# One modulation block of a diffusion layer, moved from the latent periods into the context's weight stream

## The chip, the cores and the metric

The kernel runs on one core of one Trainium2 chip. The metric is the device time of one execution in microseconds (us); the time before is the median of three runs. Engines are named as the profile names them: PE (TensorE matmuls) and PEld (its weight loads, which overlap the matmuls), DVE (VectorE), ACT (ScalarE), POOL (GpSimd), SP (SyncE, which issues nearly all DMAs). Line numbers such as L854 are lines of the kernel before.

## The reference

One layer over 512 latent tokens and 256 context tokens, width D = 2048, all in float32:

```python
mod = silu(c) @ w_ada + b_ada                  # six vectors of 2048: sh1, sc1, g1, sh2, sc2, g2
xm  = rmsnorm(x, n1) * (1 + sc1) + sh1         # latent; the context has its own sh1 and sc1
p_c = xm_ctx @ w_in[:, state columns]          # context: keys and values only
p   = xm @ w_in                                # latent: all columns
out = concat(rwkv(p, state_c), retention(p, state_c)) @ w_out
x   = x + g1 * rmsnorm(out, n2)
h   = rmsnorm(x, n3) * (1 + sc2) + sh2
y   = (silu(dwconv3x3(h @ w_gate)) * (h @ w_up)) @ w_down
x   = x + g2 * rmsnorm(y, n4)
```

The RWKV group is a delta-rule scan with one state per head and direction: the context's 256 tokens first, in four batches of heads, then the latents' 512, in eight batches, which start from the context's final states. The retention group works in chunks of 128. The modulation block that this change moves is sh2, a product of one vector of 2048 with a 2048 x 2048 matrix (16.8 MB of weights). It is needed first where h is made, long after both places where it is computed.

## The kernel before, in words

A float32 product is split in three: the weights w = hi + lo and the activations x = hi + lo, each part in a format of TensorE's single-pass matmul, and hi·hi, hi·lo and lo·hi are accumulated. The weights come through one generator, `stream` (L184). It loads a block of 4 x 128 rows (256 KB) by a DMA on SP into one of `rbufs` = 3 raw buffers, and `cut` makes hi with an ACT cast (L203) and lo with a DVE subtraction (L204) into one of `wbufs` = 3 pairs of buffers, then issues the load that refills the ring. A consumer takes one k-step of 128 rows at a time and issues its three matmuls (a triple below). Of one block, a context tile of the joint kind (`both`, L552) makes four triples of 512 and four of 256 columns, a retention tile of the context (`ret_context`, L675) four of 256, and a latent tile four of 512.

`start` makes the norms and the first products. `mixers` (L284) then runs four context batches and eight latent periods. A batch is `rw_prep`, `rw_fill` (decays, transposes, products, and the triangular solve `rw_solve` with 30 dependent steps of two DVE instructions, from the transposes of L1188 to those of L1200) and `rw_chain` (the scan). `fill` (L293) interleaves the projections' k-steps with the batch's steps in program order; how many tiles go with which batch stands in `TILES`. While the chain of one batch runs, the next batch's preparation runs beside it. The framework that builds the program then orders each engine's instructions by its own estimate of when their inputs are there, so an instruction can run far ahead of, or behind, its place in the code. At run time each engine, and SP's queue of DMA issues, goes through its list in order.

The six modulation vectors are computed in two ways. sh1 and sc1 are made on TensorE in `start`. The other four go through `ada_rest` (L828), one vector each in a different stage: a block of weights is loaded, DVE multiplies it by one element of silu(c) per partition and adds it to an accumulator (L852 opens a group, L854 continues it), and at the end of a group matmuls with a vector of ones sum over the partitions and a DVE addition puts the bias on (L859). For sh2 (`m` = 1), `mixers` opens a pool `ada2` after the context and pulls one unit (one DMA of 256 KB, 128 partitions x 512 columns, and one DVE instruction) for every `ADA` = 20 steps of projection, ten k-steps of a latent tile. There are 64 units in four groups of 16.

In the context the work pool gives the small state tiles `w` three buffers (`self.nw`, L288); the last step of a chain writes the new state into such a tile and stores it from there (L1318).

Of the kernel before, what the change touches and what calls it, by code (L numbers as in the profile page):

```python
# [9 lines left out]
F32 = mybir.dt.float32  # L10
F32R = mybir.dt.float32r
AF = mybir.ActivationFunctionType
ALU = mybir.AluOpType
# [3 lines left out]
D = 2048  # L17
KT = D // 128
# [11 lines left out]
PK_K, PK_A, PR_K, PLNW, PLNB, PW0, PA0, PNPRE, PNPOST, PFPRE, PFPOST, PCONV, PBADA, PFCB, PFCW = range(15)  # L30
# [17 lines left out]
OUT = [0.0, 1.0]  # L48
ADAR = 0.9
ADAW = 3  # L50
ADA = 20
EV = 4
ORDER = ((False, 0), (True, 2), (True, 3), (True, 0), (True, 1), (False, 1), (False, 2), (False, 3))
LAG = 2
# [13 lines left out]
def pull(steps, n=None):  # L68

    while n is None or n > 0:  # L70
        if next(steps, None) is None:
            return
        n = n and n - 1


def drain(steps):
    for _ in steps:
        pass


def merge(*streams, lead=False):


    at = [0.0] * len(streams)
    left = list(range(len(streams)))
    done = 0.0
    while left:
        i = min(left, key=lambda j: at[j])
        t = next(streams[i][0], None)
        if t is None:  # L90
            left.remove(i)
# [12 lines left out]
def fill_time(ctx):  # L104
    return 2 * (Y["d0"] + Y["d1"] + (1 if ctx else 2) * Y["d2"]) + 30 * Y["s0"] + Y["s1"] + Y["s2"] + Y["s3"] + (0 if ctx else Y["b"])


def chain_time(ctx):
    return 4 * (Y["c0"] + Y["c1"]) + 3 * Y["c2"] if ctx else 8 * (Y["c0"] + Y["c1"] + Y["c3"]) + Y["o1"] + Y["o2"]


class Kernel:
# [71 lines left out]
    def stream(self, srcs):  # L184

        nc, w = self.nc, self.wk
        blocks = (src[:, k0:k0 + w] for src in srcs for k0 in range(0, src.shape[1], w))
        raws, parts = [], []

        def load():  # L190
            src = next(blocks, None)
            if src is not None:
                n, m = src.shape[1:]
                raw = self.wp.tile([128, w, 128], F32, name="raw", bufs=self.rbufs)
                nc.sync.dma_start(raw[:, 0:n, 0:m], src)
                raws.append((raw, n, m))

        def cut():
            if raws:
                raw, n, m = raws.pop(0)  # L200
                hi = self.wp.tile([128, w, 128], F32R, name="whi", bufs=self.wbufs)
                lo = self.wp.tile([128, w, 128], F32R, name="wlo", bufs=self.wbufs)
                nc.scalar.copy(hi[:, 0:n, 0:m], raw[:, 0:n, 0:m])  # L203
                nc.vector.tensor_tensor(lo[:, 0:n, 0:m], raw[:, 0:n, 0:m], hi[:, 0:n, 0:m].bitcast(F32), op=ALU.subtract)  # L204
                parts.append((hi, lo, n, m))
                load()

        for _ in range(self.rbufs):
            load()
        for _ in range(self.wbufs - 1):  # L210
            cut()
        while parts:
            hi, lo, n, m = parts.pop(0)
            for k in range(n):
                if k == 1:
                    cut()
                yield hi[:, k, 0:m], lo[:, k, 0:m]
# [66 lines left out]
    def mixers(self, es, esw, esx, esc):  # L284

        self.done = None
        self.work, self.nt2 = self.pool(esc, "work_ctx", reuse_waits="tile"), NTC
        self.nw, self.nsv = 3, 3  # L288
        self.bw = self.pool(esc, "batch_ctx", reuse_waits="tile")
        tiles = self.ctx_tiles + self.lat_tiles  # L290
        esa, ada = ExitStack(), iter(())

        def fill(todo, *parts):  # L293

            nonlocal ada
            n, gone, done = sum(c for _, _, c in todo), 0, 0.0
            steps = chain.from_iterable(f() for _, f, _ in todo)
            for work, unit in parts:
                for t in work:
                    done += t * unit  # L300
                    while gone + 2 <= min(done, 1.0) * n:
                        t = next(steps)
                        pull(ada, (gone + t) // ADA - gone // ADA)
                        gone += t
            drain(steps)

        def take(n):
            nonlocal tiles
            todo, tiles = tiles[:n], tiles[n:]
            return todo  # L310

        nc_ = NP // 2
        prep = prep_time()
        B = self.context(0)
        drain(self.rw_prep(B))
        fill(take(TILES[0]), (self.rw_fill(B), 1 / fill_time(True)))
        for i in range(nc_):
            streams = [(self.rw_chain(B), chain_time(True), EARLYC)]
            if i + 1 < nc_:
                B = self.context(i + 1)  # L320
                streams.append((chain(self.rw_prep(B), self.rw_fill(B)), prep + fill_time(True), 1.0))
            fill(take(TILES[1 + i]), (merge(*streams, lead=True), 1.0))
        esx.close()
        esc.close()
        ap = self.pool(esa, "ada2", side="right", reuse_waits="tile")
        ada = self.ada_rest(ap, 1, 1, 2)
        self.work, self.nt2 = self.pool(es, "work", reuse_waits="tile"), NT2
        self.nw, self.nsv = NW, NSV
        self.bw = self.pool(es, "batch", reuse_waits="tile")

        self.ul = self.work.tile([128, 2, 2, 128], F32R, name="ul")
        self.nc.gpsimd.memset(self.ul.bitcast(F32), 0.0)
        batches = [self.latent(p) for p in range(NP)]
        for B, after in zip(batches, batches[1:]):
            B.next = after
        B = batches[0]
        fill(take(TILES[nc_ + 1]), (chain(self.rw_prep(B), self.rw_fill(B)), 1 / (prep + fill_time(False))))

        def period(B, p):
            streams = [(chain(self.rw_chain(B), self.rw_out(B)), chain_time(False), EARLY)]  # L340
            if p + 1 < NP:
                B = batches[p + 1]
                streams.append((chain(self.rw_prep(B), self.rw_fill(B)), prep + fill_time(False), 1.0))
            return B, merge(*streams, lead=True)

        for p in range(NP):
            todo = take(len(tiles) if p == NP - 1 else TILES[nc_ + 2 + p])
            B, steps = period(B, p)
            fill(todo, (steps, 1.0))
        pull(ada)  # L350
        esa.close()
        esw.close()
        es.close()

# [100 lines left out]
    def start(self):  # L455

        nc, a, sp = self.nc, self.a, self.sp
# [6 lines left out]
        for k in range(KT):  # L464
            for i, (pool, name, n, tag) in enumerate(kinds):
                t = pool.tile([128, n], F32, name=f"{tag}r{k}", tag=f"{tag}{k}")
# [36 lines left out]
        for k in range(KT):  # L503
# [4 lines left out]
            for i in range(len(tiles)):  # L508
                hi, lo = (w[:, k % SW] for w in ws[i])
# [3 lines left out]
                    nc.tensor.matmul(o, hi, xl, start=False, stop=False)  # L513
                    nc.tensor.matmul(o, lo, xh, start=False, stop=(last and k == KT - 1))
        first, self.ctx_tiles, self.lat_tiles = self.tiles()
        wst = self.stream([self.win(t) for ts, _, _ in first + self.ctx_tiles + self.lat_tiles for t in ts])
        self.wst = chain([next(wst)], wst)

        def out(ctx, i):
# [221 lines left out]
    def retention(self, h):  # L741
        nc, a, rp = self.nc, self.a, self.rp

        def tile(name, n=L, bufs=2):
            return rp.tile([128, n], F32, name=name, bufs=bufs)
# [9 lines left out]
        raw = []  # L755
# [28 lines left out]
        q, k = rot  # L784
# [15 lines left out]
        t = score(0)  # L800
        yield 1
        for c in range(4):
# [4 lines left out]
            t = nx  # L807
# [16 lines left out]
        nc.vector.tensor_tensor(o, po, g, op=ALU.mult)  # L824
        self.split(o, self.hh[NP + h], self.hl[NP + h])
        yield 1

    def ada_rest(self, pool, m, nk=2, bufs=3):  # L828

# [627 lines left out]
```

## Time and profile before

| | |
|---|---|
| median of three runs | 3343.24 us (3338.36 to 3350.64) |
| profiled execution, its own time | 3337.66 us |
| its span, first to last instruction | 3335.8 us |
| mean granted TensorE clock | 0.974 of 2.4 GHz |
| PE / PEld busy | 3158.3 / 2502.3 us |
| DVE / ACT / POOL busy | 2083.9 / 1121.2 / 240.6 us |
| read from HBM | 399.75 MB, 129 GB/s over the span with what is written |

The kernel's stages follow one another in the span: start to 195 us, context to about 645 us, latents to about 1500 us, retention and output projection to about 1830 us, ConvGLU to the end. A busy PE isn't a PE at its peak, since matmuls overlap and their ends are modelled.

### The profile page before, as it was taken

To read this page: it belongs to the slowest core of one execution; us is meant where nothing else is said; L and a number is where in the kernel's file an instruction comes from. 1 tells how busy PE (TensorE), PEld (TensorE's weight loads), DVE (VectorE), ACT (ScalarE), POOL (GpSimd) and SP (SyncE) were. 2 spreads that over 40 slices of the span, in tenths; PEclk is the share of its full clock that TensorE was granted. 3 is DMA by queue.
4 is the path that set the end of the run, shared out by engine and by line. 5 is a ranking of instruction groups with operands and counts; after the bars stand their busy time and mean duration, and the time that the engine had idled before them with its cause. 6 is when DMAs were issued, how large, how long until landed. Compare 5 with 4: busy or idle time off the path is not lost.

```text
span 3335.8 us, 50268 instructions
## 1 busy us (share of the span) xinstructions
PE 3158.3 (95%) x19672; PEld 2502.3 (75%) x19672; DVE 2083.9 (62%) x3562; ACT 1121.2 (34%) x1954; POOL 240.6 (7%) x382
## 2 busy tenths in 40 slices
PE   6999999989999999998998899999999999999997
PEld 3688888866767676676777688888888888788885
DVE  4474767788787878765668856335643555345544
ACT  3333245434344344333233432223322232223322
POOL 0000011101111111111210100000000000000001
PEclk9999998999999999999999899999999999999998
DMA  8832223442243433326778434333433333333342
GB/s 295 271 103 77 76 83 93 134 147 94 85 146 102 146 97 95 123 71 224 248 232 271 152 106 132 104 101 95 146 93 98 101 95 108 115 106 95 96 143 103
DMA packets 197724, 433.64 MB, mean 130 GB/s; under 512 B 25360, under 2 KB 49680, under 8 KB 197488
## 3 DMA queue, kind: packets, MB, share of 16 engines
q1 hardware_dynamic: 197488, 430.45, 40.7%
q8 instruction: 154, 2.52, 0.3%
q14 instruction: 82, 0.67, 0.1%
HBM read 399.75 MB, written 30.61 MB: 129 GB/s over the span
## 4 chain that ended last, share of the span: by engine, by line
PE 46%; DMA 4%; issue 3%; DVE 2%; POOL 1%; ACT 0%; SPq 0%; POOLq 0%; ACTq 0%; DVEq 0%
PE gbank L179 14%; PE gbank L181 14%; PE gbank L180 14%; DMA adaw<-ada 2%; DVE adacc L854 1%; POOL y L915 0%; DMA raw<-w_out 0%; DMA rxs<-ret_t 0%; DMA om<-o_mix 0%; PE gbank L903 0%; PE gbank L904 0%; PE gbank L905 0%; PE gbank L736 0%; PE gbank L737 0%; PE gbank L738 0%
## 5 line engine op out<-in xcount | busy, mean ns | idle before, releaser
L161 DVE TENSOR_TENSOR wlo<-raw,whi 128x1024 fp32r<-128x1024 f32 (+1 forms) x336 | 342.3, 1019 | 617.5 <-ACT whi L160 608.5
L160 ACT CAST whi<-raw 128x1024 fp32r<-128x1024 f32 (+1 forms) x336 | 297.2, 889 | 901.0 <-PE gbank L180 866.4
L179 PE MATMUL gbank<-hh,whi 128*128 128x512 f32 x1376 | 535.5, 389 | 0.0
L181 PE MATMUL gbank<-hh,wlo 128*128 128x512 f32 x1376 | 535.4, 389 | 0.0
L180 PE MATMUL gbank<-hl,whi 128*128 128x512 f32 x1376 | 535.3, 389 | 0.0
L203 ACT CAST whi<-raw 128x512 fp32r<-128x512 f32 (+2 forms) x320 | 210.8, 659 | 490.2 <-PE gbank L548 215.8
L549 PE MATMUL gbank<-xh,wlo 128*128 128x512 f32 (+1 forms) x896 | 368.1, 411 | 7.8 <-DVE wlo L204 7.8
L547 PE MATMUL gbank<-xh,whi 128*128 128x512 f32 (+1 forms) x896 | 368.9, 412 | 0.0
L548 PE MATMUL gbank<-xl,whi 128*128 128x512 f32 (+1 forms) x896 | 365.8, 408 | 0.0
L204 DVE TENSOR_TENSOR wlo<-raw,whi 128x512 fp32r<-128x512 f32 (+2 forms) x320 | 235.0, 737 | 106.0 <-ACT whi L203 90.1
L181 PEld LDWEIGHTS gbank<-hh,wlo 128*128 128x128 f32 x1376 | 258.3, 188 | 53.8
L180 PEld LDWEIGHTS gbank<-hl,whi 128*128 128x128 f32 x1376 | 258.3, 188 | 53.7
L179 PEld LDWEIGHTS gbank<-hh,whi 128*128 128x128 f32 x1376 | 258.3, 188 | 53.6
L181 PE MATMUL gbank<-dh,wlo 128*128 128x512 f32 x704 | 278.1, 395 | 0.4 <-DVE wlo L161 0.4
L179 PE MATMUL gbank<-dh,whi 128*128 128x512 f32 x704 | 278.0, 395 | 0.0
L180 PE MATMUL gbank<-dl,whi 128*128 128x512 f32 x704 | 277.8, 395 | 0.0
L944 DVE SCALAR_TENSOR_TENSOR cacc<-grid,fprm,cacc 128x512 f32<-128x512 f32 x352 | 264.2, 751 | 9.7 <-ACT cacc L941 1.1
L854 DVE SCALAR_TENSOR_TENSOR adacc<-adaw,sc,adacc 128x512 f32<-128x512 f32 x240 | 187.8, 783 | 74.0 <-DMA adaw<-ada 72.2
L549 PEld LDWEIGHTS gbank<-xh,wlo 128*128 128x128 f32 (+1 forms) x896 | 169.8, 190 | 51.4 <-DVE wlo L204 10.1
L547 PEld LDWEIGHTS gbank<-xh,whi 128*128 128x128 f32 (+1 forms) x896 | 170.2, 190 | 40.0 <-issue 4.8
L548 PEld LDWEIGHTS gbank<-xl,whi 128*128 128x128 f32 (+1 forms) x896 | 170.0, 190 | 37.1 <-issue 2.2
L181 PEld LDWEIGHTS gbank<-dh,wlo 128*128 128x128 f32 x704 | 132.4, 188 | 33.4 <-DVE wlo L161 1.2
(307 smaller groups left out, 4977.8 us busy)
## 6 DMA issues: line engine op xcount, KB each, us to landing
raw<-w_in SPq DMA_DIRECT2D x284, 256.0 KB, 3.0
adaw<-ada SPq DMA_DIRECT2D x192, 256.0 KB, 3.3
raw<-w_gate SPq DMA_DIRECT2D x88, 512.0 KB, 3.6
raw<-w_up_ffn SPq DMA_DIRECT2D x88, 512.0 KB, 3.6
ada<-ada SPq DMA_DIRECT2D x64, 512.0 KB, 6.1
raw<-w_down SPq DMA_DIRECT2D x64, 512.0 KB, 3.6
raw<-w_out SPq DMA_DIRECT2D x32, 512.0 KB, 5.4
adaw<-ada SPq DMA_DIRECT2D x32, 512.0 KB, 4.6
```

Source lines behind the costliest of these rows:

```text
L160: nc.scalar.copy(hi[:, 0:n, 0:m], raw[:, 0:n, 0:m])
L161: nc.vector.tensor_tensor(lo[:, 0:n, 0:m], raw[:, 0:n, 0:m], hi[:, 0:n, 0:m].bitcast(F32), op=ALU.subtract)
L179: self.nc.tensor.matmul(o, hi, xh(k), start=(k == 0), stop=False)
L180: self.nc.tensor.matmul(o, hi, xl(k), start=False, stop=False)
L181: self.nc.tensor.matmul(o, lo, xh(k), start=False, stop=(k == nk - 1))
L203: nc.scalar.copy(hi[:, 0:n, 0:m], raw[:, 0:n, 0:m])
L204: nc.vector.tensor_tensor(lo[:, 0:n, 0:m], raw[:, 0:n, 0:m], hi[:, 0:n, 0:m].bitcast(F32), op=ALU.subtract)
L547: self.nc.tensor.matmul(o, hi, xh[k], start=(k == 0), stop=False)
L548: self.nc.tensor.matmul(o, hi, xl[k], start=False, stop=False)
L549: self.done = self.nc.tensor.matmul(o, lo, xh[k], start=False, stop=(k == KT - 1))
L854: nc.vector.scalar_tensor_tensor(acc, w[:, k], c, acc, op0=ALU.mult, op1=ALU.add)
L944: nc.vector.scalar_tensor_tensor(acc, grid[:, dy:dy + 8, dx:dx + 64], cw[:, f, i:i + 1], acc, op0=ALU.mult, op1=ALU.add)
```

## The change

The units of sh2 become blocks of the weight stream while it serves the context tiles. An entry of the stream can now be a pair of a source and a function `use`; such an entry is loaded into a raw buffer like a block of weights, and when it comes to the front, `use` runs on the raw buffer in place of the cast and the subtraction, a load is issued, and the next entry is taken. The context tiles have 112 blocks. `among` leaves the first 8 and the last 8 of them alone (`AGAP`) and puts 64 units behind two of every three of the 96 between. A unit is now 2 rows of k by 256 columns, so it holds as many bytes as before (256 KB), in runs of 1 KB instead of 2 KB, and takes two DVE instructions of 256 columns instead of one of 512. There are eight groups of eight units; a group ends with two matmuls with ones and one DVE addition. The accumulator `adacc` (1 KB a partition) lives in the context's work pool, where `w` goes from three buffers to two. The pool `ada2` of the latent periods, its pulls and the constant `ADA` are gone.

```diff
-ADA = 20
+AGAP = 8, 8
@@ stream
         def cut():
-            if raws:
-                raw, n, m = raws.pop(0)
+            while raws:
+                raw, n, m, use = raws.pop(0)
+                if use:
+                    use(raw)
+                    load()
+                    continue
...
                 load()
+                break
@@ mixers
-        self.nw, self.nsv = 3, 3
+        self.nw, self.nsv = 2, 3
...
-                        t = next(steps)
-                        pull(ada, (gone + t) // ADA - gone // ADA)
-                        gone += t
+                        gone += next(steps)
...
-        ap = self.pool(esa, "ada2", side="right", reuse_waits="tile")
-        ada = self.ada_rest(ap, 1, 1, 2)
...
-        pull(ada)
-        esa.close()
@@ start
+        wst = self.stream(chain(srcs(first), self.among(srcs(self.ctx_tiles), self.ada_blocks(1)), srcs(self.lat_tiles)))
@@ new
+    def among(self, srcs, extra):
+        blocks = [src[:, k0:k0 + self.wk] for src in srcs for k0 in range(0, KT, self.wk)]
+        n = len(blocks) - sum(AGAP)
+        for i, src in enumerate(blocks):
+            yield src
+            i -= AGAP[0]
+            if 0 <= i < n:
+                yield from extra[i * len(extra) // n:(i + 1) * len(extra) // n]
+
+    def ada_blocks(self, m):
...
+                if k0 == 0:
+                    at[0] = self.work.tile([128, 256], F32, name="adacc")
+                acc = at[0]
+                for k in range(2):
+                    s = self.sc[:, k0 + k, 0:1]
+                    if k0 + k == 0:
+                        nc.vector.tensor_scalar(acc, raw[:, k], s, None, op0=ALU.mult)
+                    else:
+                        nc.vector.scalar_tensor_tensor(acc, raw[:, k], s, acc, op0=ALU.mult, op1=ALU.add)
+                if k0 == KT - 2:
+                    ps, j = self.bank(), c // 128
+                    for q in range(2):
+                        nc.tensor.matmul(ps[:, q:q + 1], acc[:, 128 * q:128 * q + 128], self.ones[:, 0:1], start=True, stop=True)
+                    nc.vector.tensor_tensor(self.mod[:, m, j:j + 2], ps[:, 0:2], b[:, 2 + m, j:j + 2], op=ALU.add)
```

## Rows read from the trace of the kernel before

**Rows 1.** Page, head: the span of the profiled execution

```profile
span 3335.8 us, 50268 instructions
```

**Rows 2.** Busy time by stage: context, latents, ConvGLU (us, times in brackets)

```profile
core 0: us, PE busy (x) PEld busy (x) DVE busy (x) ACT busy (x) POOL busy (x), PEclk, DMA share, GB/s
195.00:645.00 450.00, 427.97 (x3697) 370.06 (x3695) 309.55 (x643) 183.97 (x380) 48.37 (x111) 0.96 0.28 88
645.00:1500.00 855.00, 802.18 (x6783) 589.59 (x6779) 684.56 (x1441) 343.92 (x678) 105.59 (x207) 0.97 0.36 112
...
1830.00:3336.00 1506.00, 1471.25 (x6524) 1201.15 (x6520) 767.39 (x950) 425.89 (x544) 28.67 (x18) 0.98 0.36 111
```

**Rows 3.** Subtractions of the weights (L204), from one latent solve's end to the next

```profile
753.37:851.14 97.77, 12.88 (x19) 1.00 0.31 99
851.14:955.49 104.35, 12.90 (x19) 0.95 0.38 116
...
1052.55:1161.06 108.51, 14.55 (x21) 0.95 0.44 132
1161.06:1260.80 99.74, 12.88 (x19) 0.95 0.31 97
1260.80:1364.37 103.57, 13.59 (x20) 1.00 0.40 127
```

**Rows 4.** Modulation accumulations (L854) in three of these stretches

```profile
851.14:955.49 104.35, 7.49 (x10) 0.95 0.38 116
...
1052.55:1161.06 108.51, 11.21 (x15) 0.95 0.44 132
...
1260.80:1364.37 103.57, 8.24 (x11) 1.00 0.40 127
```

**Rows 5.** Subtractions (L204) within three latent solves, L1188 to L1200

```profile
809.21:851.14 41.93, 8.21 (x12) 1.00 0.43 135
...
1110.05:1161.06 51.01, 9.12 (x13) 1.00 0.66 198
1223.63:1260.80 37.17, 6.86 (x10) 1.00 0.45 138
```

**Rows 6.** Modulation accumulations (L854) in the second of these solves

```profile
1110.05:1161.06 51.01, 11.21 (x15) 1.00 0.66 198
```

**Rows 7.** DVE instructions by shape: count, busy us, mean ns

```profile
L854 DVE SCALAR_TENSOR_TENSOR adacc<-adaw,sc,adacc 128x512 f32<-128x512 f32 x45 | 33.6, 746 | 4.3 <-DMA adaw<-ada 3.9
L1149 DVE TENSOR_TENSOR xa<-r,t 128x256 f32<-128x256 f32 x28 | 11.7, 417 | 0.0
```

**Rows 8.** Subtractions (L204) in the context's four dense DVE stretches

```profile
228.20:261.90 33.70, 4.80 (x7) 1.00 0.22 73
...
374.10:416.00 41.90, 5.59 (x9) 1.00 0.25 81
...
468.20:517.50 49.30, 16.29 (x24) 1.00 0.43 137
...
583.50:612.00 28.50, 10.56 (x15) 0.99 0.44 137
```

**Rows 9.** Busy time of all engines, two of these and a loose stretch

```profile
228.20:261.90 33.70, 32.61 (x186) 28.41 (x186) 31.92 (x77) 7.11 (x13) 2.95 (x10) 1.00 0.22 73
261.90:374.10 112.20, 108.83 (x898) 91.52 (x897) 50.06 (x91) 39.63 (x83) 6.82 (x19) 1.00 0.24 78
...
468.20:517.50 49.30, 46.71 (x379) 44.28 (x378) 44.03 (x105) 20.73 (x39) 2.52 (x7) 1.00 0.43 137
```

**Rows 10.** The raw loads of L195 between 480 and 520 us, and who waited

```profile
L195 SPq DMA_DIRECT2D raw<-w_in x23: 327/328/777, 480.8 to 517.7; - x23
...
  ACT whi L203: 12.8, 14
...
DMA to landing us min/median/max: 2.6/2.9/4.4
```

**Rows 11.** ACT casts and DVE subtractions, 200 to 1300 us, mean ns and idle before

```profile
L204 DVE TENSOR_TENSOR wlo<-raw,whi 128x512 fp32r<-128x512 f32 (+1 forms) x237 | 160.2, 679 | 82.2 <-ACT whi L203 69.5 <-ACT tt L1226 5.2 <-PE gbank L549 3.2
L203 ACT CAST whi<-raw 128x512 fp32r<-128x512 f32 (+1 forms) x239 | 146.8, 615 | 322.7 <-PE gbank L548 161.9 <-PE obank L548 86.9 <-DMA raw<-w_in 22.7
```

**Rows 12.** The stores of the states (L1318), eight in the context

```profile
DMA to landing us min/median/max: 1.9/2.1/2.7
```

More of the change, by code (lines that the diff above doesn't have):

```diff
@@ L186, in stream, with cut_up @@
         nc, w = self.nc, self.wk
-        blocks = (src[:, k0:k0 + w] for src in srcs for k0 in range(0, src.shape[1], w))
+        def cut_up():
+            for src in srcs:
+                if isinstance(src, tuple):
+                    yield src
+                else:
+                    for k0 in range(0, src.shape[1], w):
+                        yield src[:, k0:k0 + w], None
+        blocks = cut_up()
         raws, parts = [], []
         def load():
-            src = next(blocks, None)
+            src, use = next(blocks, (None, None))
             if src is not None:
@@ L194, in load @@
                 raw = self.wp.tile([128, w, 128], F32, name="raw", bufs=self.rbufs)
-                nc.sync.dma_start(raw[:, 0:n, 0:m], src)
-                raws.append((raw, n, m))
+                raw = raw[:, 0:n, 0:m] if m <= 128 else raw.rearrange("p a b -> p (a b)")[:, 0:n * m].rearrange("p (a b) -> p a b", a=n)
+                nc.sync.dma_start(raw, src)
+                raws.append((raw, n, m, use))
         def cut():
-            if raws:
-                raw, n, m = raws.pop(0)
+            while raws:
[4 more added lines that the diff above has]
+                    continue
                 hi = self.wp.tile([128, w, 128], F32R, name="whi", bufs=self.wbufs)
                 lo = self.wp.tile([128, w, 128], F32R, name="wlo", bufs=self.wbufs)
-                nc.scalar.copy(hi[:, 0:n, 0:m], raw[:, 0:n, 0:m])
-                nc.vector.tensor_tensor(lo[:, 0:n, 0:m], raw[:, 0:n, 0:m], hi[:, 0:n, 0:m].bitcast(F32), op=ALU.subtract)
+                nc.scalar.copy(hi[:, 0:n, 0:m], raw)
+                nc.vector.tensor_tensor(lo[:, 0:n, 0:m], raw, hi[:, 0:n, 0:m].bitcast(F32), op=ALU.subtract)
                 parts.append((hi, lo, n, m))
                 load()
+                break
         for _ in range(self.rbufs):
@@ L287, in mixers @@
         self.work, self.nt2 = self.pool(esc, "work_ctx", reuse_waits="tile"), NTC
-        self.nw, self.nsv = 3, 3
+        self.nw, self.nsv = 2, 3
         self.bw = self.pool(esc, "batch_ctx", reuse_waits="tile")
         tiles = self.ctx_tiles + self.lat_tiles
-        esa, ada = ExitStack(), iter(())
         def fill(todo, *parts):
-            nonlocal ada
             n, gone, done = sum(c for _, _, c in todo), 0, 0.0
@@ L515, in start, with srcs @@
         first, self.ctx_tiles, self.lat_tiles = self.tiles()
-        wst = self.stream([self.win(t) for ts, _, _ in first + self.ctx_tiles + self.lat_tiles for t in ts])
+        def srcs(tiles):
+            return [self.win(t) for ts, _, _ in tiles for t in ts]
+        wst = self.stream(chain(srcs(first), self.among(srcs(self.ctx_tiles), self.ada_blocks(1)), srcs(self.lat_tiles)))
         self.wst = chain([next(wst)], wst)
@@ L826, in retention, with use, do @@
         yield 1
+    def among(self, srcs, extra):
+        blocks = [src[:, k0:k0 + self.wk] for src in srcs for k0 in range(0, KT, self.wk)]
+        n = len(blocks) - sum(AGAP)
+        for i, src in enumerate(blocks):
+            yield src
+            i -= AGAP[0]
+            if 0 <= i < n:
+                yield from extra[i * len(extra) // n:(i + 1) * len(extra) // n]
+    def ada_blocks(self, m):
+        nc = self.nc
+        b = self.par(PBADA).rearrange("p (m k) -> p m k", m=6)
+        at = {}
+        def use(c, k0):
+            def do(raw):
+                if k0 == 0:
[5 more added lines that the diff above has]
+                        nc.vector.tensor_scalar(acc, raw[:, k], s, None, op0=ALU.mult)
+                    else:
+                        nc.vector.scalar_tensor_tensor(acc, raw[:, k], s, acc, op0=ALU.mult, op1=ALU.add)
[4 more added lines that the diff above has]
+                    nc.vector.tensor_tensor(self.mod[:, m, j:j + 2], ps[:, 0:2], b[:, 2 + m, j:j + 2], op=ALU.add)
+            return do
+        return [(self.a["ada2"][m, c // 512, :, k0:k0 + 2, c % 512:c % 512 + 256], use(c, k0))
+                for c in range(0, D, 256) for k0 in range(0, KT, 2)]
     def ada_rest(self, pool, m, nk=2, bufs=3):
```

## The prediction

> **What bounds the kernel now.** I read the page's head first [rows 1], then the busy time by stage. Context and latents last 450 and 855 us. PE shows busy for 95% and 94% of them, DVE for 69% and 80% [rows 2]. The reader should see that no engine has the mixers to itself: PE looks nearly full in both, and DVE, idle a fifth of the latents on average, is nearly full in some stretches. So a DVE unit has to be priced by the stretch in which it stands.
>
> The latents repeat, which makes them a natural experiment. I cut them at the end of each solve and counted, per stretch, the weight blocks (subtractions) and the modulation units. The 60 later accumulations don't spread evenly, as the code pulls them, but come in bunches: two stretches with 19 blocks each and no unit last 97.77 and 99.74 us, mean 98.75; those with 10, 15 and 11 accumulations (and the opening instruction of a group in each, so 11, 16 and 12 units) last 104.35, 108.51 and 103.57 us with 19, 21 and 20 blocks [rows 3, 4]. Within a solve DVE is the pace: 37.17 us with 10 blocks and 41.93 us with 12, neither with a unit, and 51.01 us with 13 blocks and 16 units [rows 5, 6].
>
> In the context, DVE is dense in four stretches around the solves and loose between them: 31.92 of 33.70 us and 44.03 of 49.30 us busy, against 50.06 of 112.20 us [rows 9]. The stretch from 468 us belongs to the retention tiles, whose blocks are used fastest; there ACT waits for raw loads 14 times, 12.8 us in all, though each load lands in 2.9 us [rows 10]. So the ring of three raw buffers is already tight there.
>
> **The change part by part.**
>
> *Taken from the latents: 64 units, each one load and one DVE instruction of 746 ns* [rows 7], 47.7 us of DVE work. A block more costs (41.93 - 37.17)/2 = 2.4 us in a solve [rows 5]. With that taken off, the excess over 98.75 us is 5.6 us for 11 units, 9.76 - 2 x 2.4 = 5.0 us for 16, and 4.8 - 2.4 = 2.4 us for 12 [rows 3, 4]: 13.0 us for 39 units, 0.33 us each, 0.44 of the DVE time. The rest of each instruction fell where PE's projections had to be done anyway, and a shorter solve only moves them. Gain 64 x 0.33 = **21 us**. Upper end: inside the densest solve the excess over 37.17 us is 13.8 us; less three blocks at the subtraction's 0.68 us [rows 11] that is 11.8 us for 16 units, 0.74 us each, 47 us for all. Lower end: 0.20 us each, the lowest of the three stretches, 13 us. I take 0.33 because the whole stretch, not the solve, is what adds up to the total. With the units go 64 issues and buffer waits on SP's queue in the latents, in front of the loads of k, v, r; the stretch comparison holds them already. What is late next is PE with its projections.
>
> *Added to the context: 64 units of two DVE instructions.* The nearest row is a 128x256 two-source instruction, 417 ns; a pair takes 0.83 us, 12% over the one it replaces [rows 7]. A unit stands behind two of three blocks from the ninth on. The dense stretches use 7, 9, 24 and 15 blocks [rows 8]; the first holds block 7 too, so 6 count there: 54 blocks, 36 units. The other 28 fall into loose stretches, where the PE hides them: between 262 and 374 us DVE has 62 us free for 14 units' 12 us [rows 9]. For the 36 I use the same ratio as in the latents: 36 x 0.83 x 0.44 = **13 us**. Ends: 0 (projections bind there too) and the full 30 us (solve and scan are one serial path).
>
> *The ring.* In the stretch from 468 us it would carry 24 + 16 = 40 loads. A turn of a buffer is landing 2.9, cast 0.62 and subtraction 0.68, 4.2 us, so three buffers give one load every 1.4 us at best [rows 10, 11]: 56 us, where the stretch has 49.3 us [rows 8] plus 16 x 0.83 x 0.44 = 5.9. That leaves 1 us. The one from 583 us has 25 loads, 35 us, against 28.5 + 3.7, 3 us more. I take **4 us**. Behind a late raw load stand, in order, ACT's cast and the scan's copies out of PSUM on ACT, the solve's steps on DVE behind the unit, and on SP the next stores and the loads of k and v. At today's pace of 40/23 = 1.74 us a load [rows 10] it would be 69.6 + 43.5 us against 77.8, that is 35 us: the upper end. Zero if blocks slide into the scans after the solves, where PE has room.
>
> *Two buffers for w.* In a chain's last step, the second head group's new state takes the buffer from which the first's is being stored, 2.1 us to landing [rows 12], so DVE can wait once a batch: at most 8.4 us for four, nothing if the wait stands in the scan's own shadow. I take **2 us**; all other uses follow the tile before them anyway.
>
> *The rest.* A unit's rows are half as long, at as many bytes; 88 GB/s in the context [rows 2] leaves room, so no cost beyond the ring's. Eight group ends instead of four add 4 DVE additions and free as many PSUM banks late: under 2 us, taken at nothing.
>
> Sum: -21 + 13 + 4 + 2 = **-2 us**, from the profiled execution's own 3337.66 us (its span is 3335.8, rows 1) to 3335.7. That execution stands 5.6 us under the median of 3343.24; from the median it is 3341, and I say 3340 us. About 0.5%, 16.7 us, is what a measurement can tell from no change; the forecast is within it.
>
> A rule to weigh: weight loads fill 370.06 of the context's 450 us (82%), but 589.59 of the latents' 855 (69%), while the ConvGLU reaches 80% with PE alone in charge [rows 2]. The Trainium skill (Perfetto Trace Analysis, "Identifying the Most-Contended Engine") says that TensorE's headroom is to be read from the weight loads, not from matmul busy time. By it DVE would lead in the latents and PE in the context, and the sum would be -47 + 0 + 4 + 2 = -41 us. The latent stretches don't bear that out, at 0.33 us a unit.
>
> **The rivals.**
>
> A. *DVE leads the latents, PE the context.* Each unit is worth its 0.74 us in the latents, and the context hides most. For it: the solve with 16 units [rows 5, 6], and the weight loads' share. Against it: the three whole stretches [rows 3, 4]. -47 + 13 + 4 + 2 = -28 us, 3315 us. That is also the direction of the skill's rule; if the context hides all, 3302 us.
>
> B. *The ring binds in the retention tiles.* Place: 468 to 518 and 583 to 612 us. It decides once a raw load comes later than the instruction that waits for it, which already happens to 14 of 23 casts [rows 10]; a unit's first instruction is on DVE itself, in the middle of the solve, so the wait then stops the solve and not only ACT. Price: loads at 1.74 us, +35, of which half hides in the dense units' own exposure; with the DVE time in full: -21 + 30 + 18 + 2 = +29 us, 3372 us. Against it: the planner may set fewer projections into these solves and more into the scans.
>
> C. *Nothing moves for the end.* Projections bind PE in both places: gain and cost go to -13 + 8, between 3335 and 3345 us. Same verdict as the forecast, other reason.
>
> **How the numbers follow.** Forecast and C, within 0.5%: 0.44. A: 0.30; its -28 is well past 16.7 us, and the mean DVE share (69 against 80%) speaks for some gain. B: 0.26. So faster 0.30, same 0.44, slower 0.26. The two sides hold more than half, so the likeliest case's own range stands here: 3328 to 3356 us. For 8 in 10 the range takes in A at -28 and B at +29 with a little more, 3314 to 3374 us; left out are the gain with nothing paid (3302) and the full ring (DVE 30, ring 35: 3389).
>
> **What would show it.** The latent stretches between solves shrink to about 97 us at 19 blocks, all alike, and the longest solve from 51 to about 40 us; if latents shrink by 40 us or more, A holds. The context grows from 450 to about 469 us, nearly all of it from 468 us on; if 290 to 360 us grows, the units aren't hidden there. In the retention tiles' solves DVE would wait for the raw loads of the units: over 15 us of such waits there is B. Two instructions of a unit together take 0.83 us, if not, that term is mis-sized. The forecast is wrong if context and latents don't nearly cancel, or if a stage after 1500 us moves at all.

## The result: 1.6% slower, and where it went

The changed kernel takes 3399.61 us (median of four runs, 3393.61 to 3402.86) against 3343.81 us for the kernel before (four runs): a ratio of 1.0164, interval 1.014 to 1.0188, about 55 us more. The prediction said 3340 us and a range of 3314 to 3374 us; it was wrong. The two profiled executions differ by the same 56 us: 3391.8 us of span against 3335.8 [rows 1].

Lines move in the changed kernel: the load L195 is L205, the cast L203 is L217, the subtraction L204 is L218, the accumulation L854 is L862 and L864, its end L859 is L868 and L869, and the solve ends at L1247 in place of L1200.

I cut both traces at the solves' ends. The end of the first latent solve comes at 832.3 us instead of 753.4: all that is lost, and more, is lost before it, 78.9 us. From there to the last solve's end the changed kernel takes 679.8 us in place of 709.4 for the same 134 blocks, and after that 1879.8 in place of 1873.0. 78.9 - 29.6 + 6.8 is the 56 us.

The loss shows in two long stretches of the context, and in a third, shorter one between them. First the busy time of all engines in the changed kernel, by stretch (us, times in brackets, then the granted clock as a share of 2.4 GHz, the DMA share and GB/s):

```profile
core 0: us, PE busy (x) PEld busy (x) DVE busy (x) ACT busy (x) POOL busy (x), PEclk, DMA share, GB/s
300.00:325.00 25.00, 25.00 (x193) 21.38 (x192) 7.45 (x15) 6.28 (x15) 1.85 (x4) 1.00 0.22 63
325.00:361.00 36.00, 25.35 (x200) 22.65 (x199) 21.41 (x39) 8.03 (x21) 3.50 (x11) 0.62 0.09 27
361.00:395.00 34.00, 30.21 (x154) 25.74 (x154) 31.82 (x83) 7.17 (x12) 2.57 (x7) 0.85 0.46 143
...
540.00:600.00 60.00, 41.34 (x394) 33.78 (x393) 31.75 (x60) 22.61 (x55) 11.35 (x27) 0.53 0.03 8
...
641.90:730.00 88.10, 78.38 (x751) 68.94 (x752) 53.66 (x118) 34.42 (x78) 8.66 (x15) 0.92 0.53 161
```

The same view of the kernel before, the two middle stretches:

```profile
325.00:361.00 36.00, 36.00 (x263) 30.64 (x262) 13.73 (x28) 9.00 (x21) 1.50 (x5) 1.00 0.24 76
...
540.00:600.00 60.00, 56.87 (x518) 51.70 (x516) 46.89 (x96) 28.12 (x64) 14.13 (x24) 0.94 0.30 91
```

What to see: in two stretches the transfers nearly stop (27 and 8 GB/s where there were 76 and 91), and no engine is full: PE is busy for 25 of 36 and 41 of 60 us. The granted clock is 0.62 and 0.53 in the mean there, between its two levels (1.2 and 2.4 GHz) and nearer the lower. That is a wait, not work. The subtractions of the weights (L218) say what stopped:

```profile
325.00:361.00 36.00, 0.00 (x0) 0.62 0.09 27
...
482.00:502.00 20.00, 0.00 (x0) 0.97 0.24 73
...
540.00:600.00 60.00, 0.00 (x0) 0.53 0.03 8
641.90:832.30 190.40, 40.30 (x61) 0.94 0.46 141
```

In the kernel before (L204), the middle one of these and the stretch between the last context solve and the first latent one:

```profile
482.00:502.00 20.00, 7.81 (x12) 1.00 0.56 178
...
625.77:753.37 127.60, 18.06 (x29) 0.93 0.45 137
```

Not one block of weights in 36, in 20 and in 60 us; the blocks are made up later, 61 of them between the last context solve and the first latent one, where the kernel before has 29. What ends the first stop is in DVE's timeline (start, us, engine, line, operation, what it waited for):

```profile
345.71 0.69 DVE L1172 TENSOR_TENSOR t<-t,k 128x512 f32<-128x512 f32 x1 [0.36 <-ACT t L1169]
346.79 0.16 DVE L869 TENSOR_TENSOR mod<-bank,prm 128x2 f32<-128x2 f32 x1 [0.39 <-PE bank L868]
...
348.07 0.35 DVE L862 TENSOR_SCALAR adacc<-raw,sc 128x256 f32<-128x256 f32 x1
...
348.93 0.48 DVE L864 SCALAR_TENSOR_TENSOR adacc<-raw,sc,adacc 128x256 f32<-128x256 f32 x1
```

and in PE's:

```profile
344.14 1.97 PE L1207 MATMUL bank<-c_ident,t 128*128 128x128 f32 x8 [7.91 <-DVE t L1182]
345.90 0.85 PE L868 MATMUL bank<-ones,adacc 128*128 128x1 f32 x4
346.68 1.65 PE L1215 MATMUL bank<-xa,t 64*128 64x64 f32 x11
```

The group's end (L868, L869) runs at 346 us, between the transposes and the products of the next batch's preparation, and 1.3 us after it DVE opens the next group and the stream moves again. The short stop ends with L869 at 498.21 us and the second long one with L869 at 588.78 us; there PE's row names the bank's turn, since the end's matmuls are released when ACT has read out the next batch's transposes (`bkt`, L1208):

```profile
587.73 1.01 PE L868 MATMUL bank<-ones,adacc 128*128 128x1 f32 x4 [0.68 <-ACT bkt L1208]
```

At these three ends the last accumulation of the group lies 65, 51 and 69 us back. The end takes its PSUM bank from `self.bank()`, whose buffers go round in program order with the batch's preparation and solve. The stream had been running ahead of its place in the code; the end could not, because its bank's turn came after banks of a preparation that had not been reached. There is one accumulator, so the next group could not open, its loaded units stayed at the head of the three raw buffers, and every block of weights stood behind them.

### The profile page after: what moved, and what is told of

The parts are those of the page before. It is cut to its first block, busy times and chain, and to the rows that moved or that the text cites. A ratio compares the mean times of both kernels' runs of the same rounds, so it can differ in the third digit from the quotient of the medians.

```text
span 3391.8 us, 50352 instructions
## 1 busy us (share of the span) xinstructions
PE 3180.2 (94%) x19672; PEld 2522.0 (74%) x19672; DVE 2098.6 (62%) x3630; ACT 1122.8 (33%) x1955; POOL 235.0 (7%) x382
## 4 chain that ended last, share of the span: by engine, by line
PE 46%; issue 3%; DMA 3%; DVE 1%; POOL 1%; SPq 0%; ACT 0%; POOLq 0%; ACTq 0%; DVEq 0%
PE gbank L181 14%; PE gbank L179 14%; PE gbank L180 14%; DMA adaw<-ada 1%; DMA rxs<-ret_t 1%; PE bank L803 1%; DVE adacc L901 1%; POOL y L962 0%; PE gbank L557 0%; PE gbank L559 0%; POOL rtmp L791 0%; PE gbank L558 0%; PE gbank L816 0%; PE gbank L950 0%; PE gbank L951 0%
## 5 line engine op out<-in xcount | busy, mean ns | idle before, releaser
L217 ACT CAST whi<-raw 128x512 fp32r<-128x512 f32 (+2 forms) x320 | 210.7, 659 | 502.3 <-PE gbank L558 196.1
L218 DVE TENSOR_TENSOR wlo<-raw,whi 128x512 fp32r<-128x512 f32 (+2 forms) x320 | 235.3, 737 | 141.2 <-ACT whi L217 123.8
L901 DVE SCALAR_TENSOR_TENSOR adacc<-adaw,sc,adacc 128x512 f32<-128x512 f32 x180 | 140.6, 781 | 59.0 <-DMA adaw<-ada 57.8
```

Source lines behind the costliest of these rows:

```text
L217: nc.scalar.copy(hi[:, 0:n, 0:m], raw)
L218: nc.vector.tensor_tensor(lo[:, 0:n, 0:m], raw, hi[:, 0:n, 0:m].bitcast(F32), op=ALU.subtract)
L901: nc.vector.scalar_tensor_tensor(acc, w[:, k], c, acc, op0=ALU.mult, op1=ALU.add)
```

## The experiments

**The end on other banks.** One word is changed: the projections' own banks, which go round in the stream's order.

```diff
-                    ps, j = self.bank(), c // 128
+                    ps, j = self.gbank(), c // 128
```

> The changed kernel with one edit: the end of a modulation group takes its PSUM bank from the projections' own two banks (gbank) and not from the three that the batches use in turn (bank). Theory 1, the bank: in the changed trace the group ends come at 346, 495 and 588 us, long after their last accumulation, each when the next batch's fill begins; the next group can't open before (one accumulator), the raw buffers stay full, and PE has no projection at 325 to 361 and 540 to 600 us. Then the ends follow their accumulations here within some us, both gaps are gone, at least 100 weight blocks (73 in the changed kernel, 110 before) are cut by the end of the fourth context solve, and the time is that of before less about 40 us in the latents and plus 13 to 25 us for DVE and the ring in the context: 3318 to 3331 us. Theory 2, the ring of three raw buffers: at 640 to 730 us a load comes every 1.54 us and PE is at half its pace, so the lag is the ring's; the time stays over 3380 us. Theory 3, the planner sets the ends late for another reason: the ends stay late, the time stays near 3400 us.

Measured 3336.19 us, ratio to before 0.9972 (0.9959 to 0.9986). That is some 64 us under the changed kernel and 9 under the one before, and 5 us above the range that theory 1 gave. The first four ends follow the last accumulation of their group by 16, 6, 4 and 1 us, and 98 blocks are cut by the fourth context solve's end (73 in the changed kernel; at least 100 were expected). The stops are gone; all engines in the two long stretches:

```profile
325.00:361.00 36.00, 36.00 (x268) 30.86 (x267) 15.87 (x34) 9.05 (x21) 1.24 (x3) 1.00 0.39 118
540.00:600.00 60.00, 52.01 (x486) 45.11 (x483) 46.81 (x92) 28.61 (x66) 13.18 (x27) 0.93 0.35 104
```

The number of banks, of matmuls and of bytes is the same, so the stops came from the pool whose turn the end takes, and theories 2 and 3 fall. That it is the order in which this pool goes round is read from the code and from the timelines above. The Trainium skill (Perfetto Trace Analysis, "Optimization Strategy") says that a repeated gap on the engine that should be full can mean too little SBUF or PSUM for the next tile. The trace agrees with its direction, 36 and 60 us of gap behind a PSUM buffer; here it took no more of it, only another rotation.

**No ends at all.** The changed kernel with the ends left out.

```diff
-                if k0 == KT - 2:
+                if k0 == KT - 2 and c == D - 256:
+                    nc.vector.memset(self.mod[:, m], 0.0)
+                if False:
```

> The changed kernel with the eight group ends left out (no sum over partitions, no bias; sh2 is set to zero), all loads and accumulations kept. Theory 1 (the bank) and theory 3 (anything else that holds the ends): no gap in the projections, within 10 us of the run with the projections' banks, 3318 to 3331 us. Theory 2 (the ring): the loads are all there, so it stays over 3380 us.

3346.0 us, ratio 1.0000 (0.9983 to 1.0017). The stops are gone here too. It is 9 us above the kernel with the ends on the other banks, which does more, and outside both ranges, 15 us above the one of theories 1 and 3 and over 30 below that of theory 2; I have no reason for that, and it stays open. The gap matters below, where kernels without ends are compared.

**Two buffers for w, alone, in the kernel before.**

```diff
-        self.nw, self.nsv = 3, 3
+        self.nw, self.nsv = 2, 3
```

> The kernel before with two buffers in place of three for the small state tiles w in the context, nothing else. The prediction's term: 2 us slower, 0 to 8.4. If the two buffers were the cause of the changed kernel's loss, tens of us.

3344.84 us, ratio 1.0001 (0.9982 to 1.002): no difference to be seen, and an interval of 6 us to either side, so the forecast 2 us are neither shown nor excluded. Tens of us are.

**The latents without the units.** The kernel before, without the units of sh2 and nothing put in the context.

```diff
-        ada = self.ada_rest(ap, 1, 1, 2)
+        self.nc.vector.memset(self.mod[:, 1], 0.0)
+        ada = iter(())
```

> The kernel before with sh2's 64 units left out of the latents (sh2 is set to zero), nothing put in their place: the gain that the move can have at most. The prediction's term: 21 us (13 to 47), 3323 us. By the changed trace, where seven latent stretches with the same 134 blocks last 679.75 and not 709.43 us for 48 units, 0.62 us a unit: 40 us, 3304 us. If DVE paces the latents wholly: 47 us, 3296 us.

3314.59 us, ratio 0.9901 (0.9879 to 0.9924): the units were worth 33 us in the latents (25 to 40), 0.52 us each. This is the most that any other place for them can bring. The kernel with the ends on the other banks keeps 9 of it, so 24 us are paid in the context.

**The ends of the kernel before on the other banks.** In the latents the units came in bunches [rows 4]; if the bank's rotation makes the bunches, this spreads them.

```diff
-            ps = self.bank()
+            ps = self.gbank() if m == 1 else self.bank()
```

> The kernel before, with the ends of sh2's four groups in the latents on the projections' banks instead of the batches'. If the batches' banks are also what bunched the units in the latents (16 units in some 45 us, then none for 150 us), the bunches are gone here and the units come evenly, about 8 to a period. The time: the same within 10 us if DVE's time is what they cost, 10 us or more faster if the bunching was dear.

3342.97 us, ratio 0.9995 (0.9972 to 1.0017), and the bunches stayed. Accumulations (L854) by stretch:

```profile
754.00:907.00 153.00, 0.00 (x0) 0.90 0.28 84
907.00:965.00 58.00, 10.66 (x15) 1.00 0.57 179
965.00:1115.00 150.00, 0.53 (x1) 0.92 0.28 88
1115.00:1170.00 55.00, 10.94 (x15) 1.00 0.59 181
```

So the expectation failed. The ends are as late on either pool: they come 183, 150 and 171 us after the last accumulation of their group here, and 207, 144 and 171 us in the kernel before. The units run ahead until an end stops them, but it isn't the batches' banks that hold these ends; what does, no run shows. The other pool gained nothing there, and the lateness itself may well be cheap: the units of the latents had raw buffers of their own, and a unit that waits holds up no weights. That last reason is argued from the code, not shown by a run of its own.

**Loads alone.** The changed kernel without ends, each unit's DVE work cut to one instruction on 4 columns; sh2 is left at zero.

```diff
-                for k in range(2):
+                for k in range(1):
...
-                        nc.vector.scalar_tensor_tensor(acc, raw[:, k], s, acc, op0=ALU.mult, op1=ALU.add)
+                        nc.vector.scalar_tensor_tensor(acc[:, 0:4], raw[:, k, 0:4], s, acc[:, 0:4], op0=ALU.mult, op1=ALU.add)
...
```

> The changed kernel with all 64 loads of sh2 in the ring, but DVE reads only 4 columns of each row of a unit once (64 instructions of 4 columns in place of 128 of 256), and without the group ends; sh2 is set to zero. With the projections' banks the move gains 9 us net, and leaving the units out of the latents gains 33, so they cost 24 us in the context. If that is DVE's time (36 units in dense stretches at 0.96 us), the run is near 3315 us; if it is the ring (loads at 1.7 us each in the retention tiles), it stays near the 3336 to 3346 us of the runs with full units. Halves of each: 3325.

3334.15 us, ratio 0.9968 (0.9947 to 0.9988). Against the 0.9901 without any units the loads, or their place, still cost 22 us, with some 10 to either side. Of 61 us of DVE instructions (120 of 0.48 and 8 of 0.34) 14 are left here (64 of 0.22). What that brought depends on the kernel beside it. Against the one with the ends on the other banks the time fell by 1 us. The kernel that differs in DVE's work alone is the one without ends, at a ratio of 1.0000, and against it 11 us went (2 to 20 by the two intervals). So DVE's time in the context costs something between nothing and the 13 us that were forecast, or somewhat more; these runs don't settle it.

**Units earlier.** Ends on the other banks, and the units kept out of the last 64 blocks.

```diff
-AGAP = 8, 8
+AGAP = 8, 64
```

> The changed kernel with the group ends on the projections' banks, and with AGAP = 8, 64 in place of 8, 8: all 64 units behind the blocks 8 to 47, which belong to the joint tiles (4.3 us of PE a block), none behind the retention tiles' blocks (1.4 us). Ring theory: 2.6 loads a block at 1.5 us fit in 4.3 us, so the ring no longer binds, and the run is 5 to 20 us faster than with 8, 8: 3316 to 3331 us. DVE theory: 24 of the units still meet a dense solve instead of 36, some 5 us faster. If the units now crowd out the first two solves, slower than 3336 us.

3336.3 us, ratio 0.9972 (0.995 to 0.9993), the same as at their first place, where both theories asked for less. The third and fourth context solves got a little shorter or stayed (42.1 and 40.2 us, 42.8 and 43.3 at the first place), but the first two now last 42.1 and 45.1 us in place of 35.4 and 37.5: the solves beside which the units now stand got longer. ACT's waits for weights didn't fall either (65.6 us from 195 to 645 us, 39.9 at the first place).

**A ring of four.** It needs room, so a first kernel takes one of three `sv` buffers in the context (the control), and a second gives the room to the ring.

```diff
-        self.nw, self.nsv = 2, 3
+        self.nw, self.nsv = 2, 2
...
-                self.wk, self.wbufs, self.rbufs = 4, 3, 3
+                self.wk, self.wbufs, self.rbufs = 4, 3, 4
```

> Control for the next run: the changed kernel with the group ends on the projections' banks, and two in place of three buffers for the context's state tiles sv, which frees 2 KB a partition. It costs between 0 and 10 us over the 3336 us with three.

> The control with four raw buffers in the ring instead of three. Ring theory (the run in which DVE hardly read the units still paid some 20 us in the context, so the loads cost, not the DVE time): four buffers carry a load every 1.2 us or less, the fourth solve's end comes 10 us earlier or more, the retention tiles' solves cut 24 blocks or more again, and the run is 10 to 25 us faster than the control. DVE theory: the units' instructions are all there, so within 5 us of the control.

The control took 3344.73 us (1.0002, 0.9982 to 1.0023), with the ring of four 3340.28 (0.9993, 0.9972 to 1.0014). The control's two `sv` buffers cost 10 us by the ratios (2 to 18), the most that was expected. The fourth raw buffer brought 3 us, no more than the intervals allow by themselves (7 us worse to 13 better), where the ring theory asked for 10 to 25; only its lower end isn't excluded. Subtractions of the weights in the two retention stretches, first with ends on the other banks and a ring of three:

```profile
480.00:525.00 45.00, 11.03 (x16) 1.00 0.55 170
580.00:642.00 62.00, 13.08 (x19) 0.86 0.45 139
```

with the ring of four:

```profile
480.00:525.00 45.00, 12.45 (x19) 0.92 0.58 176
580.00:642.00 62.00, 13.65 (x20) 0.92 0.49 150
```

and in the kernel before:

```profile
480.00:525.00 45.00, 17.08 (x25) 0.97 0.50 158
580.00:642.00 62.00, 18.00 (x26) 0.89 0.41 128
```

With the units 16 blocks of weights go by where 25 did, and 19 where 26 did; in the control it is 16 and 19 too. The fourth buffer brings back three of the nine and one of the seven, not the 24 that the ring theory expected. A ring of four is the deepest that was tried.

**Tiny loads.** The kernel that only loads, with 2 KB a unit in place of 256 KB.

```diff
-        return [(self.a["ada2"][m, c // 512, :, k0:k0 + 2, c % 512:c % 512 + 256], use(c, k0))
+        return [(self.a["ada2"][m, c // 512, :, k0:k0 + 1, c % 512:c % 512 + 4], use(c, k0))
```

> The kernel whose units only load (group ends left out, DVE reads 4 columns once per unit, sh2 is zero) stood at 3334.15 us, 22 us above the bound of 3314.59 us that the kernel with no units at all in the latents showed wherever they would go (with a gain of 33 us against before). Here each unit's load is cut from 256 KB to 2 KB (128 partitions x 1 row x 4 columns); the number of loads, of ring slots and of issues on SP's queue stays. Theory 'slots': a unit costs because it takes one of three raw buffers for a landing and a turn, whatever its bytes: 3328 to 3338 us. Theory 'bytes': the 16.8 MB themselves delay the weight loads beside them: 3312 to 3322 us. Landing of these loads: about 2 us if most of the 2.9 us is fixed.

3331.95 us, ratio 0.9969 (0.995 to 0.9987), as with whole loads. The 16.8 MB cost nothing that can be told. The waits from 195 to 800 us (us in total, times, longest):

```profile
ACT whi L217 <- DMA raw<-w_in: 30.2, 23, 2.9
DVE adacc L864 <- DMA raw<-ada: 24.3, 13, 3.4
```

The issues in the same window (count, KB each, median us to landing):

```profile
raw<-w_in SPq DMA_DIRECT2D x136, 256.0 KB, 2.8
...
raw<-ada SPq DMA_DIRECT2D x64, 2.0 KB, 2.0
```

A load of a hundredth of the bytes still takes 2.0 us to land, and DVE still waits for it. But with whole loads these two waits were 40.9 and 36.9 us in the same window; they fell by 23 us together, and the time by no more than the intervals allow.

**A buffer of the units' own.** The control with `sv` at two, and one raw buffer for the units beside the weights' three, filled by the same call on SP's queue. The `load()` behind `use(raw)` is gone: a unit's load is now issued together with the load of the next block. In this kernel and the next two the load is L212, the cast L223, the units' accumulation L870 and the matmuls of a group's end L874.

```diff
+                if use:
+                    raw = self.wp.tile([128, w, 128], F32, name="rawu", bufs=UB)
+                else:
+                    raw = self.wp.tile([128, w, 128], F32, name="raw", bufs=self.rbufs)
...
                 if use:
                     use(raw)
-                    load()
                     continue
```

`UB` is 1.

> The kernel with group ends on the projections' banks and the context's sv buffers at two (3344.73 us; with a ring of four 3340.28), with one raw buffer of its own for the units: the weights keep their three buffers, and a unit's load is issued in the same place in SP's queue but waits only for the unit before it. Nothing is left out. Theory 'slots': the weights' ring is as deep as before the change again, so most of the loads' 22 us goes: 3322 to 3332 us. Rival 'queue': two units in a row share one buffer, and the second's load stops SP's queue, and the weight load behind it, until DVE is through with the first: 3340 to 3355 us, with DVE waiting for the units' loads for longer than the 21 us of the kernel with one ring of three.

3364.16 us, ratio 1.0064 (1.004 to 1.0087), 20 us over the control and above both ranges. SP's queue waits for units (from 195 to 800 us; us in total, times, longest):

```profile
SPq L212 <- DMA rawu<-ada: 36.9, 22, 3.6
SPq L212 <- DVE adacc L870: 36.8, 25, 6.5
```

In the control, with the units in the weights' ring, the same two waits were 27.0 and 31.4 us, so SP waits 15 us longer. ACT's wait for weights is the lowest of all these kernels, and DVE waits for the units' loads no longer than before (20.6 us); but PE itself now stands still in front of two group ends, for units that aren't through:

```profile
PE gbank L874 <- DVE adacc L870: 18.8, 2, 12.8
...
ACT whi L223 <- DMA raw<-w_in: 11.7, 8, 4.7
```

In the control that wait of PE is 0.4 us. The weights' ring is looser and the time is worse by about as much as PE stands still. So the run doesn't say what the slots of the ring are worth: a late unit now holds up PE through the end of its group, which stands in PE's list in front of the projections. The rival, SP's queue, is tried next.

**The units' loads off SP's queue,** on ACT's and on POOL's.

```diff
-                nc.sync.dma_start(raw, src)
+                (nc.scalar if use else nc.sync).dma_start(raw, src)
```

> The kernel with one raw buffer for the units beside the weights' three (3364.16 us, SP's queue waiting 37 us for DVE's unit and 37 us for the unit's landing), with the units' loads issued on ACT's queue in place of SP's. Theory 'queue' (what a unit costs is its place in SP's in-order list: a weight load waits behind a unit's load that has no buffer yet): SP's waits for units go, and the time falls to 3318 to 3335 us. Rival 'order' (a unit stands in DVE's list between steps of the solve and between two blocks' subtractions, and it is the landing of its load there that stops DVE and shifts projections out of the solves, whoever issues it): 3340 to 3370 us, with ACT now waiting in front of these loads for DVE's unit.

> The same with the units' loads on POOL's queue. Theory 'queue': 3318 to 3335 us, as with ACT, and ACT is not stopped. Rival 'order': 3340 to 3370 us; POOL itself waits long in its list for DVE (141 us for the solves' ends in the kernel before), so a unit's load behind such a wait comes late, and DVE waits for it with all behind it: above 3370 us if that decides.

3373.54 us on ACT's queue (1.0067, 1.0043 to 1.0092) and 3388.76 on POOL's (1.0116, 1.0094 to 1.0138). The first stands 4 us above the range of the rival 'order'; but the kernel before, too, ran slower beside these runs (3350.38 us), and by the ratio it is where the buffer apart was on SP's queue (1.0064). SP's queue has none of the waits for units left (0.3 us with POOL), and nothing was won. On POOL's queue the issue itself comes late, and DVE pays:

```profile
POOL rawu L212 <- DVE adacc L870: 157.7, 38, 18.9
DVE adacc L870 <- DMA rawu<-ada: 63.9, 36, 4.2
```

For the kernel with a buffer apart the theory of SP's queue falls. For the ring of three it isn't tested, since PE stands in front of group ends in these two as well (7.6 and 21.7 us), and one buffer is itself a tight ring. Of the rival 'order', the units' place in DVE's list with a landing to wait for, the run on POOL's queue bears out the late issue and DVE's wait behind it, and the one on ACT's no more than that it came out slow; the tiny loads speak against the landing's part, since DVE's waits for it fell by a third there and nothing was won. So it isn't the bytes, and a fourth buffer and another place among the blocks didn't bring it back: where the 22 us go is open.

The kernel with the ends on the projections' banks, with the units at either place, is the best that I found with all the work done, 0.3% under the kernel before.

## Why the prediction was wrong

**The step that failed** is the one under "the rest": eight group ends "free as many PSUM banks late: under 2 us, taken at nothing". The end on the batch's banks cost 64 us (3399.61 against 3336.19), more than all other terms. I had asked what the late bank costs those who want it next, and not what the end itself waits for: it takes its turn in a rotation that belongs to work the stream had outrun. And I hadn't asked what stands behind a unit that can't be used: the whole weight stream, which in the latents it never touched. In the kernel before, a sign was there to be read: the units came in bunches of 10 to 15, with stretches of none between [rows 3, 4], and I took the bunches as a natural experiment without asking what held them. An end held them, over 140 us behind its accumulations, though not by the batches' banks; that alone says that an end can come late and that the next group waits for it.

**Latents: right in kind, low in size.** The term was 21 us. The seven stretches from solve to solve, by subtractions (L218):

```profile
832.27:935.64 103.37, 12.99 (x19) 0.95 0.30 95
935.64:1028.09 92.45, 12.30 (x18) 1.00 0.32 99
...
1121.29:1216.07 94.78, 12.22 (x18) 0.96 0.32 97
1216.07:1315.67 99.60, 14.34 (x21) 1.00 0.35 105
...
sum 679.78, DVE 91.34; mean DVE 13.05
```

They last 97.1 us on average, for 19.1 blocks (97 us was forecast for 19). All alike, as said, they are not, and the number of blocks doesn't explain the rest (103.37 us with 19, 99.60 with 21). No more bunches lengthen them, and the longest solve after the first went from 51.0 to 43.0 us (40 was forecast). From 709.4 us this is 29.6 less; the 6.8 us more behind the last solve come off, since 268 blocks are done by then from 195 us on, where the kernel before has done 272. So 23 us net by these two executions, 0.36 us a unit; the runs without the units say 33, 25 to 40, or 0.52 us a unit, where 0.33 was taken. Three stretches with 39 of 64 units, corrected for blocks, were a thin base.

**The rival by the weight loads.** The rule that TensorE's headroom is to be read from its weight loads (the Trainium skill, Perfetto Trace Analysis, "Identifying the Most-Contended Engine") had led me to a rival in which DVE leads the latents, at 0.74 us a unit, and the context hides its own units. Measured were 0.52 us a unit, between that and mine. How much of DVE's time the context hid is open by these runs. The sum of -41 us didn't come, and most of what is missing is the wait at the ends.

**DVE's time in the context: not settled.** 13 us was taken. Cutting each unit's DVE work to one small instruction brought 1 us beside the kernel with ends and 11 beside the one without. The traces, one execution each, lean to the second: the first latent solve ends at 745.9 us without any units, at 765.0 with the loads alone, at 776.1 with full units and ends on the other banks, and at 784.8 with full units and no ends. One price in the term was wrong: the unit takes 2 x 480 ns, not 2 x 417. The rows, over the context:

```profile
L864 DVE SCALAR_TENSOR_TENSOR adacc<-raw,sc,adacc 128x256 f32<-128x256 f32 x84 | 40.5, 482 | 16.9 <-DMA raw<-ada 16.4
L862 DVE TENSOR_SCALAR adacc<-raw,sc 128x256 f32<-128x256 f32 x6 | 2.0, 341 | 0.1
```

**The ring: 4 us, where the loads and their place cost some 20.** Rival B named the place and the sign: waits for raw loads in the retention tiles. In the changed kernel ACT waits between 195 and 645 us:

```profile
ACT whi L217 <- DMA raw<-w_in: 58.6, 24, 6.4
```

In the kernel with the ends on the other banks it is 39.9 us, with 21.4 more of DVE for the units, where 22.7 stood before. But B's mechanism, three buffers too few, is not borne out by the fourth, which brought 3 us; the buffer apart, 20 us slower, stopped PE in another way and doesn't test it. That the pace of 1.74 us a load [rows 10] would hold was nearer than the 1.4 I took: in the 44.4 us of the kernel with the ends on the other banks from 480 us to the third solve's end 16 subtractions and 19 accumulations, so some 26 loads, make 1.71 us each.

**Two buffers for w, shorter rows.** 2 us was taken, nothing was measured that stands out of 6 us to either side. Units in rows of 1 KB landed in 2.9 us (median), no later than those in rows of 2 KB in the latents of the kernel before (3.2 us), as taken.

With the bank's rotation out of the way the forecast of -2 us stands against -9 measured (-5 to -14): the terms were wrong one by one, gains and costs both too low, and had nearly cancelled. That closeness is luck.

## What to carry to other kernels

When work joins a stream that runs ahead of its place in the code, list every buffer that it takes from a pool which others use, PSUM banks too: the stream can run ahead only as far as the slowest of these rotations. A rare, tiny step, here eight additions of 0.16 us, decides if everything behind it shares its ring. Ask of each added instruction not only what it costs and whom it delays, but what it waits for and what stands behind it. The kernels with a buffer apart show it from the other side: there the ends stood in PE's list before their units were through, and PE waited.

## What was new of the hardware

In the two long stretches without a block the granted clock was 0.62 and 0.53 of 2.4 GHz in the mean, with PE busy for 25 of 36 and 41 of 60 us. PE's batch work ran slower in them too: the matmuls of L1352 took 314 ns (median) from 560 to 588 us, at a granted clock of 0.50, the lower of the two levels, and 222 ns from 395 to 480 us, at a granted clock of 1.00. A load of 2 KB over 128 partitions landed in 2.0 us, where those of 256 KB beside it took 2.8.
